# One load of turned keys into another tile, its split at a later slot, and a later place for the memory's PV product

## The chip, the cores and the metric

The kernel runs on one core of a Trainium2 chip. Five engines of that core work side by side, each through its own list of instructions: TensorE (PE in the profile) multiplies matrices into PSUM, VectorE (DVE) and ScalarE (ACT) do the elementwise work, GpSimd (POOL) does small elementwise work and issues some transfers, SyncE (SP) issues the rest. The metric is the time of one execution on the device in microseconds (us), lower is better.

## The reference

Two layers of a decoder trunk on 256 tokens of width 1024, all in float32. Cut to what matters here:

```
for l in range(2):
    h = rms_norm(x, norm_g[l])
    q_a, k_a, v_a, q_h, f_h, i_h, q_m, z = split(h @ w_in[l])       # 1024 x 5120
    o_a = moba_attention(rope(rms_norm(q_a)), rope(rms_norm(k_a)), v_a)   # 8 heads x 64
    o_h = rms_norm(hgrn2_chunkwise(q_h, f_h, i_h, lb[l]))           # 4 heads x 128, gated linear recurrence
    k_m, v_m = split(rms_norm(mem, mem_norm_g[l]) @ w_mem_kv[l])    # 256 memory tokens
    o_m = memory_attention(rms_norm(q_m), rms_norm(k_m), v_m)       # 4 heads x 128
    y = concat([o_a, o_h, o_m]) * silu(z)                           # 256 x 1536
    x = x + y @ w_out[l]
```

With 256 tokens there is a single 256-key block, so MoBA is plain causal attention here.

## The kernel before, in words

Every large product runs in float32r with split operands: a weight tile `wr` (128 x 1024) is loaded by SP, ScalarE rounds it into a high part `wh` (L186, L189), VectorE subtracts that to get the low part `wl` (L198, L201), and TensorE adds three passes, high x high, high x low and low x high. The weights come as 120 such chunks in one fixed order, with 4 buffers for `wr` and 3 each for `wh` and `wl`. Per layer the order is: the memory's keys and values (`group_kv`, 8 chunks), then `FH` and `QH` (forget gate and query of the recurrence, `group_a`), `KA` (MoBA's keys), `IH`, `QA` (MoBA's query), `ZH`, `QM` (the memory's query), `VA`, and the gates `ZA` and `ZM`, 4 chunks each; then 12 chunks of `w_out` (`w_out_phase`), those of the recurrence first, MoBA's next, the memory's last (`KT_ORDER`).

All other work is written as Python generators. `spawn` adds one to a list; each `slot` of the matmul loops calls `step`, which moves every generator on by one; `yield n` waits n slots. So a larger number puts the instructions behind it later in the program. The framework's scheduler then orders the program by its own estimate of times; `keep_in_program_order` (used by `mm_row` too) holds an instruction at its written place. Tiles with the same `tag` share memory, so the next tile of a tag waits until the last reader of the one before is done.

Three of these generators matter here.

- `g_km` (L603) takes the memory's keys from the accumulators into `kn`, normalises them, and turns them: `across` transposes 32 x 32 blocks on VectorE into `blk` (L95), SP writes `blk` to a DRAM buffer `there` (L103) and loads it back in four pieces (L108), so that keys stand along the partitions' other axis. The pieces land in `kn` again. ScalarE then scales them into the high part `kmh` (L632) and VectorE forms the low part `kml` (L633). Their reader is the memory's score product (L1086), after `QM`.
- `g_hgrn` (L758), the recurrence. Its first product chain needs `hQ` (L696) and `hQb` (L799); TensorE's small products with them (L789, recorded at L244) are held at their written place. VectorE carries the pairs on from level to level (L775, L776) between them. Its result goes through the same turning on POOL's queue (`y_turned`), into `zh`, and is split into `yh` and `yl` (L125, L126), the first operand of `w_out`.
- The two PV products of each attention come in units `u` = 0 and 1. MoBA's (L1011) multiplies `va` with the turned probabilities `PT`, which also go through DRAM on POOL's queue. The memory's (L1138) multiplies `vmh` and `vml` with `mP`; its first matmul is held at its written place, which the `yield 4` at L1131 sets. Both write one of four PSUM buffers `sd`; `y_store` (L738) multiplies with the gate and splits the result for `w_out`.

Of the kernel before, what the change touches and what calls it, by code (L numbers as in the profile page):

```python
# [12 lines left out]
F32 = mybir.dt.float32  # L13
F32R = mybir.dt.float32r
# [3 lines left out]
AF = mybir.ActivationFunctionType  # L18
OP = mybir.AluOpType
# [26 lines left out]
def hymba_kernel(ctx: ExitStack, tc: tile.TileContext, x, mem, mem_t, positions, w_in, w_out, w_mem_kv,  # L46
                 gains, moba_g, out):
    nc = tc.nc
    cst = ctx.enter_context(tc.tile_pool(name="cst", bufs=1))
    sb = ctx.enter_context(tc.tile_pool(name="sb", bufs=1))  # L50
# [13 lines left out]
    def room(what, n=1):  # L64
        while held[what] + n > room_of[what]:
            yield
# [9 lines left out]
    def side_tile():  # L76
        held["sd"] += 1
        assert held["sd"] <= 4
        return psum.tile([128, 512], F32, name="sd", tag="sd", bufs=4)

    def rel(what="sd", n=1):
        held[what] -= n

    def small(name, n):
        return sb.tile([128, n], F32, name=name, tag=name, bufs=2)


    def across(dst, src, n, stage=None, free=None, name=None, q=None):
        q = q or nc.sync
        if stage is None:  # L90
            yield from room("blk")
            held["blk"] += 1
        tag = stage or "blk"
        blk = sb.tile([128, 4, n * 32], F32, name="blk", tag=tag, bufs=1)
        nc.vector.transpose(blk.rearrange("p c (n i) -> p c n i", n=n),  # L95
                            src.rearrange("p (n c i) -> p c n i", n=n, c=4))
        if free is not None:
            rel(free)
        if name is not None:
            done.add(name)  # L100
        yield 2
        there = away.tile([4, 32, 4, n * 32], F32, name="there", tag="there", bufs=2)
        q.dma_start(there.rearrange("q j c r -> (q j) c r"), blk)  # L103
        if stage is None:
            rel("blk")
        yield 4
        for c in range(4):
            q.dma_start(dst[c * 32:c * 32 + 32], there[:, :, c].rearrange("q j r -> j q r"))  # L108
            if c == 1:
                yield  # L110

    def turned(a, stage=None, q=None):
        yield from across(a.rearrange("p (q r) -> p q r", q=4), a, 8, stage, q=q)
        yield 5

    def strips(a):
        return a.rearrange("p (q t h i) -> p h t q i", q=4, t=2, h=4)
# [91 lines left out]
    done = set()  # L209
# [29 lines left out]
    def mm(o, a, b, s, e):  # L239
        nc.tensor.matmul(o, lhsT=a, rhs=b, start=s, stop=e)  # L240
# [347 lines left out]
    def heads(t, n):  # L588
        return t.rearrange("p (h d) -> p h d", h=n)

    def sumsq(dst, acc, n):
        sq = sb.tile([128, 512], F32, name="sq", tag="sq", bufs=2)
        nc.scalar.activation(sq, acc, AF.Square)
        nc.vector.tensor_reduce(dst, heads(sq, n), AX.X, OP.add)
# [8 lines left out]
    def g_km(l, acc):  # L603
        ss = small("ssk", 8)
        kn = sb.tile([128, 2, 512], F32, name="kn", tag="qk", bufs=1)
        nc.vector.tensor_copy(kn[:, 0], acc[0])
        nc.scalar.copy(kn[:, 1], acc[1])  # L607
        yield
        for t in range(2):
            sumsq(ss[:, t * 4:t * 4 + 4], kn[:, t], 4)  # L610
        yield
        while "rm" not in done:
            yield
        ms = small("msk", 8)
        for t in range(2):
            nc.vector.tensor_scalar(ms[:, t * 4:t * 4 + 4], ss[:, t * 4:t * 4 + 4], rm2[:, t:t + 1], EPS,
                                    op0=OP.mult, op1=OP.add)
        r = small("rk", 8)
        nc.gpsimd.tensor_tensor(r, ms, pw[:, :8], op=OP.pow)
        for t in range(2):  # L620
            nc.gpsimd.tensor_scalar(r[:, t * 4:t * 4 + 4], r[:, t * 4:t * 4 + 4], rm[:, t:t + 1], None, op0=OP.mult)
        yield 3
        for t in range(2):
            nc.vector.tensor_tensor(heads(kn[:, t], 4), heads(kn[:, t], 4),
                                    r[:, t * 4:t * 4 + 4][:, :, None].to_broadcast([128, 4, 128]), op=OP.mult)
        yield 3
        kmh = sb.tile([128, 1024], F32R, name="kmh", tag="kmh", bufs=1)
        kml = sb.tile([128, 1024], F32R, name="kml", tag="kml", bufs=1)
        g = gkq[:, l:l + 1]
        flat = kn.rearrange("p t s -> p (t s)")  # L630
        yield from turned(flat)
        nc.scalar.activation(kmh, flat, AF.Copy, scale=g)  # L632
        nc.vector.scalar_tensor_tensor(kml, in0=flat, scalar=g, in1=kmh.bitcast(F32), op0=OP.mult, op1=OP.subtract)  # L633
        T["km"] = kmh, kml
        done.add(f"km{l}")

# [437 lines left out]
    def g_mem_unit(l, u, qm, r, nr):  # L1074
        km, vm = T["km"], T["vm"]
        passes = ((0, 1), (1, 0), (0, 0))
        if u == 0:
            yield from room("P")
            held["P"] += 1
        P = sb.tile([128, 2, 2, 256], F32, name="P", tag=("P", "qk")[u], bufs=2 - u)  # L1080
        yield from room("sd", 2)
        ps = [side_tile() for _ in range(2)]
        for t in range(2):
            for i in range(2):
                for a, b in passes:
                    mm(ps[t][:, i * 256:(i + 1) * 256].rearrange("p (t q s) -> p t q s", t=2, q=4),  # L1086
                       qm[a][:, 2 * u + i, t * 128:(t + 1) * 128], strips(km[b])[:, 2 * u + i],
                       (a, b) == passes[0], (a, b) == passes[2])
        done.add(f"scores{u}{l}")
        yield  # L1090
        mx = small("mxm%d" % u, 4)
        nb = small("nbm%d" % u, 4)
        sm = small("smm%d" % u, 4)
        ri = small("rim%d" % u, 4)
        for t in range(2):
            nc.vector.tensor_reduce(mx[:, 2 * t:2 * t + 2], heads(ps[t], 2), AX.X, OP.max)
        nc.vector.tensor_tensor(nb.rearrange("p (t h) -> p t h", t=2), mx.rearrange("p (t h) -> p t h", t=2),
                                nr.rearrange("p (t h) -> p t h", t=2)[:, :, 2 * u:2 * u + 2], op=OP.mult)
        yield
        for t in range(2):  # L1100
            for i in range(2):
                c, cr = 2 * t + i, 4 * t + 2 * u + i
                T["exp"] = nc.scalar.activation(P[:, t, i], ps[t][:, i * 256:(i + 1) * 256], AF.Exp,
                                     bias=nb[:, c:c + 1], scale=r[:, cr:cr + 1], accum_out=sm[:, c:c + 1])
            rel()
            yield
        if u:
            done.add(f"exps{l}")
        yield
        nc.vector.reciprocal(ri, sm)  # L1110
        for t in range(2):
            for i in range(2):
                c = 2 * t + i
                nc.vector.tensor_scalar(P[:, t, i], P[:, t, i], ri[:, c:c + 1], None, op0=OP.mult)
        yield 5
        while f"scores1{l}" not in done:
            yield
        PT = [sb.tile([128, 2, 2, 256], F32R, name="mP", tag=n, bufs=1) for n in (("hF", "kmh"), ("ih", "kml"))[u]]
        for b in range(2):
            yield from room("sd")  # L1120
            pt = side_tile()
            for i in range(2):
                for t in range(2):
                    nc.tensor.transpose(pt[:, i * 256 + t * 128:i * 256 + (t + 1) * 128],
                                        P[:, t, i, b * 128:(b + 1) * 128], ident)
            nc.scalar.copy(PT[0][:, b], heads(pt, 2))
            nc.vector.tensor_tensor(PT[1][:, b], heads(pt, 2), PT[0][:, b].bitcast(F32), op=OP.subtract)
            rel()
        if u == 0:
            rel("P")  # L1130
        yield 4  # L1131
        yield from room("sd")
        po = side_tile()
        for i in range(2):
            hs = slice((2 * u + i) * 128, (2 * u + i + 1) * 128)
            for b in range(2):
                for x, y in passes:
                    (mm if i or b or x != passes[0][0] or y != passes[0][1] else mm_row)(po[:, i * 256:(i + 1) * 256], vm[x][:, b, hs], PT[y][:, b, i],  # L1138
                       b == 0 and (x, y) == passes[0], b == 1 and (x, y) == passes[2])
        yield  # L1140
        while f"z{M_}{l}" not in done:
            yield
        y_store(l, M_, u, po)
# [130 lines left out]
```

## Time and profile before

| | |
|---|---|
| median of 3 runs | 399.3 us (398.44 to 402.74) |
| the profiled execution | 402.14 us, of which the span of its instructions is 400.3 us |
| TensorE busy | 390.2 us (97%) |
| VectorE, ScalarE, GpSimd busy | 314.6, 250.8, 69.7 us |
| mean granted TensorE clock | 0.999 |
| moved by DMA | 80.33 MB, 201 GB/s |

TensorE is busy almost throughout, so a microsecond can only be won where TensorE waits, or at the ends of the span. The profile names each such wait by the instruction that waited and the one that released it.

### The profile page before, as it was taken

To read this page: it belongs to the slowest core of one execution; us is meant where nothing else is said; L and a number is where in the kernel's file an instruction comes from. 1 tells how busy PE (TensorE), PEld (TensorE's weight loads), DVE (VectorE), ACT (ScalarE), POOL (GpSimd) and SP (SyncE) were. 2 spreads that over 40 slices of the span, in tenths; PEclk is the share of its full clock that TensorE was granted. 3 is DMA by queue.
4 is the path that set the end of the run, shared out by engine and by line. 5 is a ranking of instruction groups with operands and counts; after the bars stand their busy time and mean duration, and the time that the engine had idled before them with its cause. 6 is when DMAs were issued, how large, how long until landed. Compare 5 with 4: busy or idle time off the path is not lost.

```text
span 400.3 us, 7603 instructions
## 1 busy us (share of the span) xinstructions
PE 390.2 (97%) x2871; PEld 326.3 (82%) x2871; DVE 314.6 (79%) x606; ACT 250.8 (63%) x422; POOL 69.7 (17%) x109
## 2 busy tenths in 40 slices
PE   8999998999999999899999999999999999989996
PEld 6888887778888888788888888788888889878885
DVE  4789969998559997974576689799866799788543
ACT  5998754646768849644375665455855894875340
POOL 2013400703202514000000040031050061300000
PEclk9999999999999999999999999999999999999999
DMA  7976684368533989726565558554854188981612
GB/s 277 412 281 228 233 213 159 111 210 252 169 106 149 245 288 297 232 86 203 185 196 174 180 189 251 179 176 165 270 187 145 59 265 256 331 245 54 207 56 105
DMA packets 24900, 80.33 MB, mean 201 GB/s; under 512 B 3232, under 2 KB 5664, under 8 KB 24864
## 3 DMA queue, kind: packets, MB, share of 16 engines
q1 hardware_dynamic: 22304, 71.31, 53.5%
q0 software_dynamic: 2272, 8.39, 8.1%
q8 instruction: 22, 0.36, 0.4%
q10 hardware_dynamic: 288, 0.15, 0.1%
q14 instruction: 14, 0.11, 0.1%
HBM read 72.51 MB, written 7.34 MB: 199 GB/s over the span
## 4 chain that ended last, share of the span: by engine, by line
PE 73%; DMA 8%; DVE 8%; issue 4%; POOL 3%; ACT 2%; SPq 1%; ACTq 0%; DVEq 0%; POOLq 0%
PE acc L240 47%; PE acc L1160 16%; PE sd L240 5%; DMA kn<-there 4%; PE sd L244 3%; DMA zh<-there 3%; DVE wl L198 2%; POOL PT L108 1%; POOL rka L900 1%; PE sd L453 1%; DVE blk L95 1%; POOL zh L108 1%; DMA gT<-in_gains_dram 1%; DMA there<-blk 1%; ACT wh L186 1%
## 5 line engine op out<-in xcount | busy, mean ns | idle before, releaser
L198 DVE TENSOR_TENSOR wl<-wr,wh 128x1024 fp32r<-128x1024 f32 x96 | 116.7, 1218 | 42.6 <-ACT wh L186 42.5
L186 ACT CAST wh<-wr 128x1024 fp32r<-128x1024 f32 x96 | 100.5, 1050 | 66.1 <-PE acc L240 35.3
L240 PE MATMUL acc<-wh,hT 128*128 128x512 f32 x384 | 124.8, 396 | 0.0
L240 PEld LDWEIGHTS acc<-wh,hT 128*128 128x128 f32 x384 | 71.8, 188 | 16.1 <-issue 0.7
L240 PE MATMUL acc<-wl,hT 128*128 128x512 f32 x192 | 75.2, 392 | 0.7 <-DVE wl L198 0.7
L240 PE MATMUL acc<-hT,wh 128*128 128x512 f32 x256 | 65.3, 393 | 0.0
L240 PEld LDWEIGHTS acc<-hT,wh 128*128 128x128 f32 x256 | 45.8, 189 | 8.2 <-ACT kn L607 0.4
L240 PEld LDWEIGHTS acc<-wl,hT 128*128 128x128 f32 x192 | 36.1, 188 | 7.9 <-DVE wl L198 1.0
L240 PEld LDWEIGHTS acc<-hT,wl 128*128 128x128 f32 x256 | 35.2, 190 | 2.5
L1160 PE MATMUL acc<-wl,yh 128*128 128x512 f32 (+1 forms) x96 | 37.2, 387 | 0.0
L1160 PE MATMUL acc<-wh,yl 128*128 128x512 f32 (+1 forms) x96 | 36.6, 388 | 0.0
L240 PE MATMUL acc<-hT,wl 128*128 128x256 f32 x256 | 36.6, 283 | 0.0
L201 DVE SCALAR_TENSOR_TENSOR wl<-wr,gT,wh 128x1024 fp32r<-128x1024 f32 (+1 forms) x29 | 31.2, 1097 | 6.7 <-ACT wh L189 6.3
L189 ACT ACTIVATE wh<-wr,gT 128x1024 fp32r<-128x1024 f32 (+1 forms) x29 | 28.6, 1002 | 10.9 <-PE acc L240 4.0
L1160 PE MATMUL acc<-wh,yh 128*128 128x512 f32 (+1 forms) x96 | 30.7, 390 | 2.5 <-ACT yh L125 2.5
L240 PE MATMUL acc<-wh,mTh 128*128 128x512 f32 x64 | 25.4, 401 | 0.2 <-DVE mTh L392 0.2
L240 PE MATMUL acc<-wh,mTl 128*128 128x512 f32 x64 | 25.2, 397 | 0.0
L1160 PEld LDWEIGHTS acc<-wh,yh 128*128 128x128 f32 x96 | 18.0, 188 | 6.6 <-ACT yh L125 3.0
L986 ACT ACTIVATE P<-P,nba,rq 128x128 f32<-128x128 f32 (+1 forms) x32 | 17.1, 536 | 8.3 <-DVE nba L980 8.3
L1160 PEld LDWEIGHTS acc<-wh,yl 128*128 128x128 f32 x96 | 18.0, 188 | 3.8 <-issue 0.2
L1160 PEld LDWEIGHTS acc<-wl,yh 128*128 128x128 f32 x96 | 18.0, 188 | 3.6
L240 PE MATMUL acc<-wl,mTh 128*128 128x512 f32 x64 | 20.2, 392 | 0.0
(222 smaller groups left out, 574.6 us busy)
## 6 DMA issues: line engine op xcount, KB each, us to landing
wr<-in_w_in_dram SPq DMA_DIRECT2D x80, 512.0 KB, 4.2
wr<-in_w_out_dram SPq DMA_DIRECT2D x24, 512.0 KB, 4.6
wr<-in_w_mem_kv_dram SPq DMA_DIRECT2D x15, 512.0 KB, 4.4
there<-blk POOLq DMA_DIRECT2D x4, 768.0 KB, 4.7
PT<-there POOLq DMA_DIRECT2D x16, 192.0 KB, 7.2
there<-blk SPq DMA_DIRECT2D x4, 512.0 KB, 3.1
xs<-in_x_dram SPq DMA_DIRECT2D x2, 512.0 KB, 8.8
memr<-in_mem_dram SPq DMA_DIRECT2D x2, 512.0 KB, 6.7
```

The costliest lines, as they stand in the source:

```text
L95: nc.vector.transpose(blk.rearrange("p c (n i) -> p c n i", n=n), src.rearrange("p (n c i) -> p c n i", n=n, c=4))
L108: q.dma_start(dst[c * 32:c * 32 + 32], there[:, :, c].rearrange("q j r -> j q r"))
L186: nc.scalar.copy(whs[i], raws[i])
L189: nc.scalar.activation(whs[i][:, sl], raws[i][:, sl], AF.Copy, scale=gT[:, g:g + 1])
L198: nc.vector.tensor_tensor(wls[i], raws[i], whs[i].bitcast(F32), op=OP.subtract)
L201: ins = nc.vector.scalar_tensor_tensor(wls[i][:, sl], in0=raws[i][:, sl], scalar=gT[:, g:g + 1], in1=whs[i][:, sl].bitcast(F32), op0=OP.mu ...
L240: nc.tensor.matmul(o, lhsT=a, rhs=b, start=s, stop=e)
L244: tc.keep_in_program_order(nc.tensor.matmul(o, lhsT=a, rhs=b, start=s, stop=e))
L453: ins = nc.tensor.transpose(pt[:, j * 256 + t * 128:j * 256 + (t + 1) * 128], xn[t][:, k * 128:(k + 1) * 128], ident)
L900: nc.gpsimd.tensor_tensor(r[:, t8], ms[:, t8], pw[:, :8], op=OP.pow)
L986: nc.scalar.activation(P[:, i, kc[t]], P[:, i, kc[t]], AF.Exp, bias=nb[:, c:c + 1], scale=rq[:, r:r + 1], accum_out=sm[:, c:c + 1])
L1160: ins = nc.tensor.matmul(a, lhsT=y, rhs=wt[:, cs], start=n == (0 if to is None else nk - 2) and j == 0, stop=n == nk - 1 and j == 2)
```

## The change

In `g_km` the four pieces of the turned keys are loaded into `kt`, a float32 tile in the memory that `kml` has, instead of back into `kn`. ScalarE's scaling and VectorE's subtraction read `kt`; the subtraction writes its result over its own input. Both no longer follow five slots after the load: they wait until `g_ih` has marked the recurrence's input as taken over (`ih{l}`, during `QA`), and five more slots, and are held at that written place. In `g_mem_unit` the memory's PV product stands eight slots after its probabilities instead of four.

```
-        kml = sb.tile([128, 1024], F32R, name="kml", tag="kml", bufs=1)
+        kt = sb.tile([128, 1024], F32, name="kml", tag="kml", bufs=1)
+        kml = kt.bitcast(F32R)
         g = gkq[:, l:l + 1]
-        flat = kn.rearrange("p t s -> p (t s)")
-        yield from turned(flat)
-        nc.scalar.activation(kmh, flat, AF.Copy, scale=g)
-        nc.vector.scalar_tensor_tensor(kml, in0=flat, scalar=g, in1=kmh.bitcast(F32), op0=OP.mult, op1=OP.subtract)
+        yield from across(kt.rearrange("p (q r) -> p q r", q=4), kn.rearrange("p t s -> p (t s)"), 8)
+        while f"ih{l}" not in done:
+            yield
+        yield 5
+        tc.keep_in_program_order(nc.scalar.activation(kmh, kt, AF.Copy, scale=g))
+        tc.keep_in_program_order(nc.vector.scalar_tensor_tensor(kml, in0=kt, scalar=g, in1=kmh.bitcast(F32),
+                                                                op0=OP.mult, op1=OP.subtract))
...
         if u == 0:
             rel("P")
-        yield 4
+        yield 8
         yield from room("sd")
         po = side_tile()
```

The numbers of lines behind L635 grow by four (L799 becomes L803, L1160 becomes L1164). What this does to the order on three engines, layer 0:

On VectorE, near the end of `QH`, the row of `kml` stood ahead of the recurrence's `hQ` and `hQb`. Before:

```order
L324 TENSOR_TENSOR as<-acc,al 128x256
L511 SCALAR_TENSOR_TENSOR rt<-rt 128x16
L633 SCALAR_TENSOR_TENSOR kml<-kn,gkq,kmh 128x1024
L504 TENSOR_SCALAR rt<-rt 128x16
L696 TENSOR_TENSOR hQ<-as,sg 128x512
L505 TENSOR_SCALAR rt<-rt 128x16
L198 TENSOR_TENSOR wl<-wr,wh 128x1024
L799 TENSOR_TENSOR hQb<-hQ,hF 128x1024
```

Now the same stretch, where `rt` are small steps of the rotary angles:

```order
L324 TENSOR_TENSOR as<-acc,al 128x256
L511 SCALAR_TENSOR_TENSOR rt<-rt 128x16
L504 TENSOR_SCALAR rt<-rt 128x16
L505 TENSOR_SCALAR rt<-rt 128x16
L506 TENSOR_SCALAR rt<-rt 128x16
L700 TENSOR_TENSOR hQ<-as,sg 128x512
L511 SCALAR_TENSOR_TENSOR rt<-rt 128x16
L803 TENSOR_TENSOR hQb<-hQ,hF 128x1024
```

The row of `kml` has gone from here, `hQb` stands ahead of the next `wl`, and the small rotary steps have moved forward.

On ScalarE the row of `kmh` now stands during `ZH`, after the two squares of MoBA's query (`sq`) and ahead of `hX`, a copy for the recurrence's output:

```order
L593 ACTIVATE sq<-acc 128x512
L186 CAST wh<-wr 128x1024
L635 ACTIVATE kmh<-kml,gkq 128x1024
L863 COPY hX<-sd 128x512
L186 CAST wh<-wr 128x1024 x2
```

VectorE's row of `kml` follows there too, ahead of a `wl`; both layers have it so.

On TensorE, at the start of `w_out`, unit 0 of the memory's PV (`mP`) came first, then four rows of `w_out` (`yh`), then the memory's unit 1 with MoBA's unit 0 (`PT`) inside it. Before:

```order
L240 MATMUL sd<-mP,vmh 128x256
L1160 MATMUL acc<-wh,yh_1991 128x512
L1160 MATMUL acc<-wl,yh_1991 128x512
L1160 MATMUL acc<-wh,yh_1991 128x512
L1160 MATMUL acc<-wl,yh_1991 128x512
L244 MATMUL sd<-mP,vmh 128x256
L240 MATMUL sd<-mP,vml 128x256
L240 MATMUL sd<-mP,vmh 128x256
L244 MATMUL sd<-PT,va 64x256
L240 MATMUL sd<-PT,va 64x128
```

Now MoBA's unit 0 stands ahead of the memory's unit 0, and both ahead of `w_out`:

```order
L240 MATMUL sd<-PT,va 64x256
L240 MATMUL sd<-PT,va 64x128
L244 MATMUL sd<-mP,vmh 128x256
L240 MATMUL sd<-mP,vml 128x256
L240 MATMUL sd<-mP,vmh 128x256 x2
L240 MATMUL sd<-mP,vml 128x256
L240 MATMUL sd<-mP,vmh 128x256 x2
L240 MATMUL sd<-mP,vml 128x256
L240 MATMUL sd<-mP,vmh 128x256 x2
L240 MATMUL sd<-mP,vml 128x256
L240 MATMUL sd<-mP,vmh 128x256
L1164 MATMUL acc<-wh,yh_1991 128x512
```

Eight matmuls with `PT` have moved ahead of the first row of `w_out`; the memory's unit 1 has moved behind some 30 rows of `w_out`, and MoBA's unit 1 stands alone between rows 8 and 9 of it. Layer 1 has the same shape, with MoBA's unit 1 after row 6.

## The prediction

> **What bounds the kernel now.** The page comes first: which engine is full, and at what clock.
>
> ```profile
> span 400.3 us, 7603 instructions
> PE 390.2 (97%) x2871; PEld 326.3 (82%) x2871; DVE 314.6 (79%) x606; ACT 250.8 (63%) x422; POOL 69.7 (17%) x109
> PEclk9999999999999999999999999999999999999999
> PE 73%; DMA 8%; DVE 8%; issue 4%; POOL 3%; ACT 2%; SPq 1%; ACTq 0%; DVEq 0%; POOLq 0%
> ```
>
> TensorE is busy in 97% of the span at full clock, and the change neither adds nor removes a matmul. So only TensorE's waits can be won: 400.3 - 390.2 = 10.1 us are not busy, start and end included. The last line says that the chain of work that ended last runs over TensorE for 73% only; the rest passes through transfers and VectorE, so some waits are on that chain. The view of waits for TensorE names them (total, times, longest):
>
> ```profile
> PE acc L1160 <- ACT yh L125: 2.5, 2, 1.5
> PE sd L244 <- DVE hQb L799: 1.5, 2, 1.0
> ...
> PE acc L240 <- DVE wl L198: 0.7, 1, 0.7
> PE sd L244 <- DVE hKb L776: 0.5, 1, 0.5
> ```
>
> That is 5.2 us in four kinds, and the timeline of TensorE gives their places (start, duration, and idle time ahead in brackets):
>
> ```profile
> 61.95 0.76 PE L244 MATMUL sd<-hQb,hK 128*32 128x32 f32 x64 [1.01 <-DVE hQb L799]
> ...
> 80.51 0.50 PE L240 MATMUL acc<-wl,hT 128*128 128x512 f32 x1 [0.72 <-DVE wl L198]
> ...
> 88.35 0.65 PE L244 MATMUL sd<-hQ,hKb 128*32 128x64 f32 x32 [0.54 <-DVE hKb L776]
> ...
> 257.72 0.76 PE L244 MATMUL sd<-hQb,hK 128*32 128x32 f32 x64 [0.50 <-DVE hQb L799]
> ...
> 164.38 0.50 PE L1160 MATMUL acc<-wh,yh 128*128 128x512 f32 x1 [1.05 <-ACT yh L125]
> ...
> 358.86 0.50 PE L1160 MATMUL acc<-wh,yh 128*128 128x512 f32 x1 [1.49 <-ACT yh L125]
> ```
>
> Three stand in layer 0 behind the recurrence's first product (1.01 + 0.72 + 0.54 = 2.27), one at the same place in layer 1 (0.50), and one at each start of `w_out` (1.05 + 1.49 = 2.54). Sum 5.31. The first four lead back, on the chain, to the load of the turned keys:
>
> ```profile
> 44.68 2.97 DMA there<-blk
> ...
> 48.99 7.31 DMA kn<-there
> ...
> 244.75 6.86 DMA kn<-there
> ```
>
> and on ScalarE and VectorE, in order of time, to the two instructions that read it:
>
> ```profile
> 56.40 1.15 ACT L632 ACTIVATE kmh<-kn,gkq 128x1024 fp32r<-128x1024 f32 x1 [3.88 <-DMA kn<-there]
> 57.59 1.28 DVE L633 SCALAR_TENSOR_TENSOR kml<-kn,gkq,kmh 128x1024 fp32r<-128x1024 f32 x1 [3.54 <-ACT kmh L632]
> 60.68 1.22 DVE L799 TENSOR_TENSOR hQb<-hQ,hF 128x1024 f32<-128x1024 f32 x1
> ...
> 252.87 1.28 DVE L633 SCALAR_TENSOR_TENSOR kml<-kn,gkq,kmh 128x1024 fp32r<-128x1024 f32 x1 [2.71 <-ACT kmh L632]
> ```
>
> VectorE stood still for 3.54 us with `hQ` and `hQb` queued behind `kml`; TensorE needed `hQb` 1.01 us before it came.
>
> **Part 1, the split moves: four waits go.** In layer 0 the idle 3.54 and the instruction's own 1.28 us leave the stretch, so VectorE can be up to 4.82 us earlier at `hQb`. ScalarE's `sg`, which `hQ` needs, no longer queues behind `kmh` either. TensorE would want VectorE 2.27 us earlier up to 88.35, so 4.82 covers it with 2.5 to spare; beyond that VectorE is held by the `wh` of the chunks, which TensorE paces. VectorE's other work there is the same, only in another order: the rotary steps come early, and POOL makes the rotary table before its two slow powers. In layer 1 it is 2.71 + 1.28 = 3.99 against 0.50. I take both as won whole: **2.77 us**; the ends are 0 (POOL's powers hold VectorE instead) and 2.77.
>
> **Where the two instructions go.** They now stand in `ZH`, ahead of the rows below. The load has landed some 40 us earlier by then, so they wait for nothing; behind them on ScalarE stand `hX` and the next `wh`, behind them on VectorE the next `wl`.
>
> ```profile
> 97.02 0.58 ACT L859 COPY hX<-sd 128x512 f32<-128x512 f32 x1
> 99.69 1.05 ACT L186 CAST wh<-wr 128x1024 fp32r<-128x1024 f32 x1 [2.09 <-PE acc L240]
> ...
> 103.50 1.22 DVE L198 TENSOR_TENSOR wl<-wr,wh 128x1024 fp32r<-128x1024 f32 x1 [1.50 <-ACT wh L186]
> ...
> 115.04 2.68 PE sd L240 x24
> ...
> 171.12 31.07 PE acc L1160 x136
> ```
>
> ScalarE has 2.09 us of idle time behind `hX` for its 1.15; VectorE gives 1.28 out of 1.50. `hX`, which TensorE reads in the stretch from 115.04 on, was ready at 97.6, so 1.15 later is free. Cost **0**; without that cover it is at most 1.28 per layer, which is the upper end. The four loads themselves keep their place on SP's queue; they only write another tile, whose last reader in layer 0 is nothing and in layer 1 the memory's unit 1 of layer 0: at 31.07 / 136 = 0.23 us a row it ends some 30 rows and three PV products behind 164.4, near 175, against a load near 240. Cost 0, both ends.
>
> **Part 2, MoBA's unit 0 moves into the wait.** The start of `w_out` is set by `zh`:
>
> ```profile
> 132.44 2.24 POOL L108 DMA_DIRECT2D PT<-there  x4 [1.54 <-PE acc L240]
> ...
> 157.02 0.56 POOL L108 DMA_DIRECT2D zh<-there  x1 [2.52 <-issue]
> ...
> 157.02 6.60 DMA zh<-there
> 163.71 0.63 ACT yh L125
> ...
> 351.98 6.11 DMA zh<-there
> DMA to landing us min/median/max: 5.6/7.2/9.2
> ```
>
> The last row is that of `PT`: issued until 134.7 and landing at most 9.2 us later, unit 0's probabilities are there by 143.9, long before TensorE is done with `ZM` and takes up the memory's unit 0, at 161.73 in the next rows. So the moved matmuls wait for nothing. Their length:
>
> ```profile
> 161.73 0.28 PE L244 MATMUL sd<-mP,vmh 128*128 128x256 f32 x1
> ...
> 163.05 0.28 PE L240 MATMUL sd<-mP,vmh 128*128 128x256 f32 x1
> ...
> 165.86 0.43 PE L244 MATMUL sd<-PT,va 128*64 128x256 f32 x1
> ...
> 167.36 0.39 PE L240 MATMUL sd<-mP,vmh 128*128 128x256 f32 x1
> ```
>
> 167.36 - 165.86 = 1.50 us. Layer 0's wait of 1.05 is filled whole (TensorE then comes 0.45 after `yh`, less the 0.17 of a matmul's ordinary spacing); layer 1's 1.49 is filled to within nothing. I take 1.05 + 1.49 = **2.54 us**, provided `zh` comes earlier by as much as TensorE does. For that, one row of busy times (TensorE, weight loads, VectorE, ScalarE, POOL) and two of the timeline: from 120 to 142 VectorE is full on the way to `zh` and `PT`, but the work that leads into this stretch waits for TensorE:
>
> ```profile
> 120.00:142.00 22.00, 22.00 (x117) 18.82 (x116) 21.96 (x60) 16.31 (x35) 7.75 (x8) 1.00 0.72 202
> ...
> 104.69 0.59 ACT L936 COPY qT<-sd 128x512 f32<-128x512 f32 x1 [0.73 <-PE sd L935]
> 107.22 0.69 DVE L719 TENSOR_TENSOR zh<-acc,sg 128x512 f32<-128x512 f32 x1 [2.49 <-ACT sg L717]
> ```
>
> So the stretch begins earlier by what TensorE has won, and `zh` follows. The memory's unit 1 comes some 7 us later; its result is wanted by the last third of `w_out`, some 66 rows of 0.23 us behind. Cost 0; the upper end is in the third rival.
>
> **The sum.** 2.77 + 2.54 = 5.31. I keep 0.7 of it back for waits this small that shift rather than go: the new order leaves the low part `yl` a few tenths only before its first reader, at both starts of `w_out`. Gain **4.6 us**. The profiled execution took 402.14 (span 400.3 and 1.84 around it), so 397.5 on its own footing. It stands 2.84 above the median of 399.3. If a profiled run carries that always, the median becomes 394.7. For this speaks that the waits recur alike in both layers, so they are not one run's accident.
>
> A rule of the Trainium skill speaks against part 2. "DMA: Bandwidth & Descriptors", in "Anatomy of one DMA", fits POOL-issued transfers as 2.0 us and bytes at 436 GB/s; by it the last piece of `zh` (128 KB) would land about 2.3 us after its issue, an estimate, ahead of TensorE, part 2 would win nothing, and the sum would be 2.77 alone, 396.5. The trace disagrees: 6.60 and 6.11 us.
>
> **The rivals.**
> 1. *The waits were larger in the profiled execution than in the median one.* Landing times of `kn` (7.31, 6.86) and `zh` set them, and transfers vary: the three runs spread over 4.3 us while TensorE's work is fixed. Then the change reaches a floor that the median had half reached: 402.14 - 5.31 = 396.8. Against it: the like waits in both layers. 0.24. The rule of the skill's page would be the extreme of this case, with its 396.5.
> 2. *`zh` does not follow TensorE.* VectorE is full from 120 to 142; if its own work and not its start sets the end, `w_out` starts when it does now, and what is won ahead of it is given back as a longer wait. Each layer then wins only the 1.50 of unit 0, which no longer stands behind: 3.0, hence 396.3. A new hold in layer 0 (VectorE waiting for POOL's powers at `kr`) gives about the same, 5.31 - 2.27 = 3.0. 0.18.
> 3. *Slower: `zh` comes later.* TensorE runs ahead, and the loads of weights crowd the same 16 DMA engines as `PT` and `zh`. The fourth piece of `zh` is issued when the first piece of unit 1's `PT` has landed (the 2.52 us marked issue), so both latencies count. At the 9.2 of the view instead of 6.60 and 6.11 the last piece costs 2.6 and 3.1 us, and the `PT` piece ahead of it up to 3.0 and 2.2 more: 10.9 in all, less 5.3, so 399.3 + 5.6 = 404.9. It decides from 5.3 us over both layers on. Against it: the rows are from the same crowded stretches. 0.08.
> 4. *It does not do what it says*, and the scheduler's new order trades one wait for another: within 1 us of 399.3. 0.06.
>
> **How the numbers follow.** The forecast holds 0.44, with 394.7; its own range is 393.4 (all 5.31 and another 0.1 us of slower restart behind each of six waits) to 396.8. The range over the cases is 393.4 to 399.0: it leaves out the third rival and part of the fourth. About 1% (4.0 us) can be told from no change in this kernel: faster than 395.3 is most of the forecast and a little of the first two rivals, 0.44; slower than 403.3 is the third rival, 0.07; the rest, 0.49.
>
> **What would show it.** In the changed profile TensorE's waits on `hQb`, `hKb` and `wl` should be gone in both layers; `kmh` should have no wait on a transfer and stand near 97 and 289; TensorE should pass from `ZM` through `PT` and `mP` into `yh` with under 0.3 us idle. It is wrong if the wait on `yh` stays over 1 us (rival 2 or 3), if VectorE waits for POOL at `kr` near 68, or if TensorE waits for the fourth chunk's `wh` or `wl` in `w_out`, whose buffers come free only with chunk 0's last row, now about a dozen rows later.

## The result, and the profile after

| | before | after |
|---|---|---|
| median | 402.3 us (20 runs, 398.44 to 407.19) | 396.43 us (20 runs, 395.34 to 399.69) |
| ratio | | 0.9877, 95% interval 0.9852 to 0.9902 |
| the profiled execution | 402.14 us | 399.69 us, the longest of its 20; a second one 398.48 us |

The change wins 1.2%, some 5 us by the ratio and 5.9 by the medians. (A ratio, here and below, is over the fast executions alone, those within 1.5% of the kernel's lowest time; a median is over all of them.) The forecast was 394.7 us; the range held the time. The 399.3 us of the three runs shown before lay 3 us under what the same kernel does over many runs (402.3 here; 402.11, 402.28 and 402.33 beside the experiments).

The page of the profile after, in the places that answer to those of before:

```profile
span 397.9 us, 7596 instructions
PE 390.5 (98%) x2871; PEld 326.1 (82%) x2871; DVE 314.6 (79%) x606; ACT 251.1 (63%) x422; POOL 70.3 (18%) x109
PE 86%; DMA 4%; DVE 4%; POOL 2%; issue 2%; ACT 1%; SPq 0%; ACTq 0%; DVEq 0%; POOLq 0%
```

TensorE's share of the chain that ended last has gone from 73 to 86%; DMA and VectorE have 4% each instead of 8%. The view of waits for TensorE:

```profile
PE acc L1164 <- ACT yh L125: 2.0, 1, 2.0
PE sd L240 <- DVE dm L368: 1.0, 1, 1.0
PE acc L240 <- DVE mTh L392: 0.3, 1, 0.3
PE acc L240 <- ACT wh L189: 0.2, 1, 0.2
PE sd L244 <- ACT wh L186: 0.2, 1, 0.2
```

The lines on `hQb`, `hKb` and `wl` are gone; `dm`, `mTh` and `wh` belong to the first 9 us of the program, and the last line is all that is left in the recurrence. TensorE's timeline has the three places of layer 0 where it waited before, then the way from `ZM` to the start of `w_out`, then the start of `w_out` in layer 1:

```profile
60.73 0.71 PE L244 MATMUL sd<-hQb,hK 128*32 128x32 f32 x62
...
78.38 0.49 PE L240 MATMUL acc<-wl,hT 128*128 128x512 f32 x1
...
85.82 0.65 PE L244 MATMUL sd<-hQ,hKb 128*32 128x64 f32 x32 [0.17 <-ACT wh L186]
...
159.28 0.43 PE L244 MATMUL sd<-PT,va 128*64 128x256 f32 x1
...
160.78 0.39 PE L244 MATMUL sd<-mP,vmh 128*128 128x256 f32 x1
...
162.31 0.40 PE L1164 MATMUL acc<-wh,yh 128*128 128x512 f32 x1
...
356.51 0.79 PE L1164 MATMUL acc<-wh,yh 128*128 128x512 f32 x1 [2.01 <-ACT yh L125]
```

Rows without a bracket waited for nothing. In layer 0 TensorE goes from `ZM` through `PT` and `mP` into `yh` without a pause, 2.45 us earlier than before at the first row behind `ZM` (161.73 there). In layer 1 of this execution it waits longer than before, 2.01 instead of 1.49. A second profile of the same kernel has it the other way round, a wait in layer 0 and none in layer 1:

```profile
164.74 0.50 PE L1164 MATMUL acc<-wh,yh 128*128 128x512 f32 x1 [1.84 <-ACT yh L125]
...
353.83 0.43 PE L244 MATMUL sd<-PT,va 128*64 128x256 f32 x1
...
356.87 0.40 PE L1164 MATMUL acc<-wh,yh 128*128 128x512 f32 x1
```

The chains of the two executions name the reason, the last piece of `zh` (start, duration to landing). The first execution, layer 1, then the second, layer 0:

```profile
345.52 10.21 DMA zh<-there
```

```profile
156.38 7.59 DMA zh<-there
```

Before it took 6.60 and 6.11. In the first execution the piece itself took long, and so did its three neighbours (13.0 to 13.3 us); in the second it was also issued late, 5.4 us behind the first piece of `zh` (150.98) where it was 4.2 before, since it is the eighth transfer of GpSimd's queue and came only when the first piece of `PT` had landed. So the cover of part 2 is enough where `zh` lands as before, and some executions have a landing that goes beyond it. Both profiled executions have the longest time of their group, while 16 of the 20 runs lie between 395.3 and 397.0. The same is true of all three runs below that have both parts in another form: whether the profiled execution is longer because it is profiled, or by its place in the run, is not known.

A sum without these two waits: in the chains, layer 0 can be followed from a row near 24 us, behind the program's start, and layer 1 begins with the second row shown. Before,

```profile
24.25 19.25 PE acc L240 x103
...
202.19 10.66 PE acc L240 x47
```

and now:

```profile
24.21 36.03 PE acc L240 x188
...
198.36 10.66 PE acc L240 x47
```

From equal starts (24.25 and 24.21) that is 3.8 us for layer 0, where 2.27 + 1.05 = 3.32 were predicted. For layer 1 the second execution, which did not wait there, has 191.8 us from its chain's same row to TensorE's last one, the profile before 194.2: 2.4 us, where 0.50 + 1.49 = 1.99 were predicted. Together 6.2, and 402.14 - 6.2 = 395.9, where most runs are.

```profile
200.89 10.66 PE acc L240 x47
...
392.70 0.28 PE L1164 MATMUL sd<-wh,yl 128*128 128x256 f32 x1
```

(Before, the second of these rows starts at 396.39.) That is 0.9 us more than the six idle times, and the timelines place it. Up to the first row behind `ZM` the layers have become 2.41 and 0.64 us shorter (137.48 to 135.07, 153.58 to 152.94) where 2.27 and 0.50 were idle: 0.28 more. From there to the layer's end, with the waits taken off, 39.41 has become 39.08 and 39.13 has become 38.87: another 0.59 for the same matmuls in another order.

### The profile page after: what moved, and what is told of

Its sections match the earlier page's. It is cut to its first block, busy times and chain, and to the rows that moved or that the text cites. A ratio compares the mean times of both kernels' runs of the same rounds, so it can differ in the third digit from the quotient of the medians.

```text
span 397.9 us, 7596 instructions
## 1 busy us (share of the span) xinstructions
PE 390.5 (98%) x2871; PEld 326.1 (82%) x2871; DVE 314.6 (79%) x606; ACT 251.1 (63%) x422; POOL 70.3 (18%) x109
## 4 chain that ended last, share of the span: by engine, by line
PE 86%; DMA 4%; DVE 4%; POOL 2%; issue 2%; ACT 1%; SPq 0%; ACTq 0%; DVEq 0%; POOLq 0%
PE acc L240 58%; PE acc L1164 17%; PE sd L240 5%; PE sd L244 3%; DMA zh<-there 3%; DMA wr<-in_w_mem_kv_dram 1%; DVE wl L198 1%; PE sd L453 1%; ACT wh L186 1%; POOL rka L904 1%; POOL PT L108 0%; PE sd L1068 0%; PE sd L939 0%; PE sd L1128 0%; POOL rtB L548 0%
## 5 line engine op out<-in xcount | busy, mean ns | idle before, releaser
L1164 PE MATMUL acc<-wl,yh 128*128 128x512 f32 (+1 forms) x96 | 37.7, 392 | 0.0
L1164 PE MATMUL acc<-wh,yl 128*128 128x512 f32 (+1 forms) x96 | 37.1, 392 | 0.0
L1164 PE MATMUL acc<-wh,yh 128*128 128x512 f32 (+1 forms) x96 | 30.4, 396 | 2.0 <-ACT yh L125 2.0
L1164 PEld LDWEIGHTS acc<-wh,yh 128*128 128x128 f32 x96 | 18.3, 190 | 6.1 <-ACT yh L125 2.2
L1164 PEld LDWEIGHTS acc<-wh,yl 128*128 128x128 f32 x96 | 18.3, 191 | 3.8
L1164 PEld LDWEIGHTS acc<-wl,yh 128*128 128x128 f32 x96 | 18.3, 191 | 3.6
```

The lines of the kernel that those rows point to most:

```text
L1164: ins = nc.tensor.matmul(a, lhsT=y, rhs=wt[:, cs], start=n == (0 if to is None else nk - 2) and j == 0, stop=n == nk - 1 and j == 2)
```

## The experiments

Each part was run by itself, against the prices of 2.77 us for the split and 2.54 us for the cover, and against the rival that `zh` does not follow.

### The split alone (two runs)

The change, with the memory's PV in `g_mem_unit` at its old place:

```
-        yield 8
+        yield 4
```

> The split of kn alone: new tile and late place as in the change, but the memory's PV four slots behind its probabilities as before, so that the start of w_out has its old order on TensorE. My theory (the four waits behind the load go whole, and zh follows TensorE): the waits on hQb, hKb and wl are gone, the wait for yh stays at 1.0 to 1.3 us in layer 0 and near 1.5 in layer 1, and the time falls by 2.8 us, ratio 0.993. Rival 2 (zh does not follow): the same waits go, but the wait for yh grows to about 3.3 us in layer 0 and 2.0 in layer 1, ratio 1.000. If the median execution has smaller waits than the profiled one: 0.995 to 0.998.

Measured: 401.47 us at the median (398.0 to 406.3 without the profiled execution), ratio 0.9971, 0.9936 to 1.0006. The profiled execution of this run was out of order as a whole (1366.95 us), so the kernel was run again for its profile.

> The split of kn alone once more, now to see its profile: its runs fell into a group near 398.4 and one near 401.8 us. Theory A (the gate): TensorE waits for yh at the start of w_out some 1.5 to 2.5 us in one layer or both, and where the wait fills more than half of one window of 3.41 us the clock is 0.50 in the window behind it, which costs 1.7 us more each time; ratio again 0.996 to 0.998. Theory B (zh does not follow, no gate): the wait grows to 3.3 and 2.0 us and the clock stays at 1.00.

Measured: 401.0 us, ratio 0.9954, 0.9916 to 0.9993; the profiled execution took 399.09. Its waits, without those of the first 9 us and 0.17 us on a `wh`:

```profile
PE acc L1164 <- ACT yh L125: 2.1, 2, 1.6
```

The waits behind the load are gone, and in this execution (1.64 and 0.42 us at `yh`) `zh` has followed; the clock stayed at 1.00. So neither A nor B is what the profile shows. Yet of the 2.77 us the median gained only 0.6 in the first run and 1.3 in the second (1.2 and 1.9 by the ratios), and it lies 2 us above the execution that was profiled. What the other executions lose had to be found by taking suspects away.

### The place of the memory's PV alone

The kernel before, with this one line of the change:

```
-        yield 4
+        yield 8
```

> The PV's place alone: split of kn as before, the memory's PV eight slots behind its probabilities, so that MoBA's unit 0 stands ahead of w_out. My theory (MoBA's unit 0 fills the wait for zh, 1.05 and 1.49 us): the wait for yh goes in both layers, the waits on hQb, hKb and wl stay as they were, the time falls by 2.5 us, ratio 0.994. If the two parts only pay together (the cover needs part 1): 1.000. If nearly all of the whole gain comes from here, since a late zh also costs clock: 0.989 to 0.991.

Measured: 399.42 us, ratio 0.9959, 0.9921 to 0.9998; 2.7 us at the median and 1.6 by the ratio, beside the 2.54 of the sum. TensorE's waits behind the first 9 us:

```profile
PE acc L1160 <- ACT yh L125: 2.0, 1, 2.0
PE sd L244 <- DVE hQb L799: 0.6, 1, 0.6
PE sd L244 <- DVE hKb L776: 0.6, 1, 0.6
PE acc L240 <- DVE wl L198: 0.5, 1, 0.5
```

Behind `kml` three of the four waits are there (layer 0's on `hQb` is missing in this execution), and the wait for `yh` has left layer 0. In layer 1 this execution, too, met a late `zh`.

By the ratios the split alone gives 1.2 to 1.9 us, the PV's place 1.6, both together 4.9. That they pay more together than apart is suggested by this and not shown: each ratio has an interval of some 1.5 us either way.

### Only the tile

The kernel before, with `kt` as in the change and the two instructions at their old place:

```
-        yield from turned(flat)
-        nc.scalar.activation(kmh, flat, AF.Copy, scale=g)
-        nc.vector.scalar_tensor_tensor(kml, in0=flat, scalar=g, in1=kmh.bitcast(F32), op0=OP.mult, op1=OP.subtract)
+        yield from across(kt.rearrange("p (q r) -> p q r", q=4), kn.rearrange("p t s -> p (t s)"), 8)
+        yield 5
+        nc.scalar.activation(kmh, kt, AF.Copy, scale=g)
+        nc.vector.scalar_tensor_tensor(kml, in0=kt, scalar=g, in1=kmh.bitcast(F32), op0=OP.mult, op1=OP.subtract)
```

> Only the tile: the turned keys land in kml's tile and the two instructions read it, at the old place in the program (five slots behind the load, not held), all else as before. My theory (only the place counts, the tile is a means): VectorE still stands 3 us or more in front of kml with hQb behind it, ratio 1.000 within 0.002. Rival (the target of the load matters, because loading into kn waits for its last reader): the load of the pieces starts earlier or lands sooner, and a part of the 2.8 us goes, ratio 0.995 or less.

Measured: 402.79 us, ratio 1.003, 0.9998 to 1.0063. ScalarE and VectorE still stand in front of the landing, with the queue behind them:

```profile
55.62 1.15 ACT L633 ACTIVATE kmh<-kml,gkq 128x1024 fp32r<-128x1024 f32 x1 [2.58 <-DMA kml<-there]
56.81 1.29 DVE L634 SCALAR_TENSOR_TENSOR kml<-kml,gkq,kmh 128x1024 fp32r<-128x1024 f32 x1 [2.25 <-ACT kmh L633]
```

The rival falls: the tile by itself brings nothing. Keeping `kn` as the load's target with a late split was not tried, because MoBA's keys take over `kn`'s memory in between.

### The split soon behind the load, alone and with part 2

The split alone, with another place for it:

```
-        while f"ih{l}" not in done:
-            yield
-        yield 5
+        yield 9
```

> The tile, with the split held nine slots behind the load and no waiting for the recurrence's input: kml stands on VectorE behind the first hQb (two levels further on) in KA, some 40 us earlier than in the change; the memory's PV as before. My theory (what counts is that hQ and hQb no longer stand behind the load; how far the split moves is indifferent): like the split alone, ratio 0.993. Rival (the late place counts, because VectorE has no room for 1.28 us in the recurrence's levels): TensorE waits on hQb or hKb of a later level by up to 1.3 us in each layer, ratio 0.996 to 1.000.

Measured: 398.93 us, ratio 0.9914, 0.9875 to 0.9954, with

```profile
PE acc L1162 <- ACT yh L125: 2.1, 2, 1.5
```

as the only wait of TensorE behind the start. The interval overlaps those of the late split (0.9971, 0.9954), so a difference is not shown. With the PV's new place besides:

> The split nine slots behind the load, held (as in the run of that name, 0.991 alone), with the memory's PV eight slots behind its probabilities as in the change. If the place of the split does not matter as long as it is behind hQb: the same as the change, ratio to before 0.986 to 0.989. If the late place in ZH costs something on the way to zh (the split alone gave 0.997 there, against 0.991 here): 1 to 2 us below the change, ratio 0.982 to 0.985.

Measured: 396.19 us, ratio 0.9857, 0.9811 to 0.9903, the change's own time. As far as these runs can tell, how late the split stands does not matter; that it stands behind `hQb` does. (The profiled execution, 398.18 us, waited 1.49 us for `yh` in layer 1.)

### The new place's cover

The change, with two more instructions between its own two:

```
+        tc.keep_in_program_order(nc.scalar.activation(kmh, kt, AF.Copy, scale=g))
+        ex = sb.tile([128, 1024], F32R, name="ex", tag="ex", bufs=1)
+        tc.keep_in_program_order(nc.vector.scalar_tensor_tensor(ex, in0=kt, scalar=g, in1=kmh.bitcast(F32),
+                                                                op0=OP.mult, op1=OP.subtract))
```

> The change, with both instructions of the split issued twice at their new place: a second kmh (the same values) and a second low part into a tile of its own, so 1.15 us more on ScalarE and 1.28 more on VectorE in each layer. The prediction put the cost of the new place at 0, because ScalarE is idle for 2.09 us behind hX and VectorE for 1.50 ahead of wl there. If the cover holds with room: the same as the change within 0.5 us, ratio 0.985 to 0.989. If the cover is already used up: up to 1.28 us a layer on TensorE's path, 398 to 399, ratio 0.990 to 0.993, and the profile shows TensorE waiting for wh, wl or hX between 95 and 120 us.

Measured: 396.39 us, ratio 0.9859, 0.9824 to 0.9894. VectorE and ScalarE did the work twice,

```profile
94.49 1.15 ACT L635 ACTIVATE kmh<-kml,gkq 128x1024 fp32r<-128x1024 f32 x1
...
96.01 1.15 ACT L636 ACTIVATE kmh<-kml,gkq 128x1024 fp32r<-128x1024 f32 x1
```

```profile
98.38 1.28 DVE L638 SCALAR_TENSOR_TENSOR ex<-kml,gkq,kmh 128x1024 fp32r<-128x1024 f32 x1
...
100.71 1.28 DVE L640 SCALAR_TENSOR_TENSOR kml<-kml,gkq,kmh 128x1024 fp32r<-128x1024 f32 x1
```

and TensorE waited for nothing between 95 and 120 us. The cover holds with room for as much again. (At `yh` in layer 1 this execution, 397.41 us, waited 1.25.)

### Is it the clock? Matmuls of zeros in the wait

Two profiles (below, on the hardware) show a stretch of half clock behind a wait for `yh` of 2.0 us. If such stretches make up what the split alone loses (theory A), keeping TensorE busy in the wait must win it back. The split alone, and in `w_out_phase`, ahead of the first rows:

```
+            if n == 0:
+                for _ in range(10):
+                    mm_row(acc[0][0][:, :256], zb[:, :128], zb)
```

> The split of kn alone, and ten matmuls of zeros (128x256, about 0.11 us each, 1.1 in all) into an accumulator just ahead of the memory's unit 0 at each start of w_out; they change no result, for the first row of w_out starts that accumulator anew. They do nothing for the time at which yh is there. Theory A (a part of the price of the late zh is the clock that falls after it): TensorE is idle 1.1 us less, the clock does not fall any more, and the time is 1.5 to 2.5 us below that of the split alone, ratio to before 0.991 to 0.993, with a narrower spread. Theory B (only the wait counts): the same as the split alone where the wait is over 1.1 us, and up to 1.1 us per layer more where it is shorter: 0 to 1.5 us above the split alone.

Measured: 400.88 us (399.57 to 404.25), ratio 0.9988, 0.9955 to 1.002, beside 401.0 (from 397.74) and 0.9954 for the split alone in the same session. The lowest time rose by 1.8 us, nearly the ten matmuls' length over two layers (1.03 us a layer in the profile), and the median did not move. So the gain of 1.5 to 2.5 us that theory A asked for did not come, and theory B's numbers fit.

The clock is not cleared by this, for the record has the mean granted clock of every execution. Of 23 executions of the split alone, 13 have a clock of 0.996 or less; none has 0.997. The medians of these 13 are 402.0 and 401.7 us in the two runs, those of the others 398.6 and 399.1. One window at half clock, 1.7 us in 400, is 0.4%. With the ten matmuls only 2 of 12 are so low. The falls went, as theory A has it, but the ten matmuls cost an execution without a fall 1.6 to 2.1 us (the median of such executions is now 400.7), and the median of all stays. So the median execution of the split alone loses a wait and a window of half clock behind it, and this experiment does not part the two.

### zh ahead of PT on GpSimd's queue

The direct test of a late `zh` is to make it early. In `across` the four loads of unit 1's `PT` come three slots later (`lag` is 7 for it and 4 for all others) and are held there; the product with `PT` keeps its slot, since its own `yield 13` becomes 10:

```
-        yield 4
+        yield lag
...
-            q.dma_start(dst[c * 32:c * 32 + 32], there[:, :, c].rearrange("q j r -> j q r"))
+            ins = q.dma_start(dst[c * 32:c * 32 + 32], there[:, :, c].rearrange("q j r -> j q r"))
+            if pin:
+                tc.keep_in_program_order(ins)
```

First with the whole change, then with the split alone, then with the kernel before.

> The change, and the four loads of unit 1's PT are issued three slots later and held there, so that the four loads of zh stand ahead of them on GpSimd's queue. The scheduler then takes four rows of w_out ahead of MoBA's unit 0. If the late fourth piece of zh, which waits for the first piece of PT to land, is what is left at the start of w_out: zh lands 3 to 4 us earlier, no wait on yh is left, MoBA's unit 1 gets its PT in time, and the time is 0 to 1 us below that of the change (ratio to before 0.984 to 0.987), with no run near 399. Rival: the bytes on the DMA engines set the landing, not the order of issue: zh lands hardly earlier, the four rows that now come first wait, and TensorE then waits for PT as well, 0.5 to 3 us above the change.

Measured: 395.98 us (395.74 to 396.71), ratio 0.9839, 0.9793 to 0.9886. GpSimd's timeline and TensorE's first row of `w_out` in layer 1:

```profile
150.32 2.24 POOL L108 DMA_DIRECT2D zh<-there  x4 [6.45 <-DMA there<-blk]
152.72 1.67 POOL L108 DMA_DIRECT2D PT<-there  x3 [0.17 <-issue]
155.48 0.56 POOL L108 DMA_DIRECT2D PT<-there  x1 [1.09 <-issue]
```

```profile
351.98 0.40 PE L1166 MATMUL acc<-wh,yh 128*128 128x512 f32 x1
```

Now the eighth transfer, the one held back, is a piece of `PT`; `zh` has landed 2.7 to 2.9 us before TensorE takes up `yh`, and the row waits for nothing, in either layer. No run is over 396.71. This is the lowest median of all; 0.4 to 0.6 us below the change's medians is less than these runs can tell.

> The split of kn alone (the memory's PV four slots behind its probabilities), and the four loads of zh ahead of those of unit 1's PT on GpSimd's queue. The split alone gave 401.2 at the median, though its profile (399.09) shows 2.06 us of waiting for yh and a floor of 397.0. Theory C (in the median execution the rest up to 401 is waiting for a late zh): with zh early it goes without part 2 of the change, 396 to 397, ratio 0.984 to 0.987, narrow. Theory D (the rest is somewhere else): only the 2.06 go, 399 to 399.5, ratio 0.991 to 0.993.

Measured: 397.25 us (396.9 to 397.66), ratio 0.9881, 0.985 to 0.9912. Theory C has the cause right and the number a little low: without part 2, 3.8 of the split's 401.0 us go (2.9 by the ratios), though its profile showed only 2.06 us of waiting. No execution has a clock of 0.996 or less any more, so what goes is the wait and the half clock behind it. TensorE's waits behind the first 9 us are down to one line:

```profile
PE sd L246 <- ACT wh L188: 0.2, 1, 0.2
```

It still lies 1.3 us over the same with part 2, where neither waits for `yh`. Most of this is the order of the rows in `w_out`: from its first row to the row with which layer 1 begins, the chain's second one below, the split with `zh` first takes 39.66 us,

```profile
159.73 0.40 PE L1166 MATMUL acc<-wh,yh 128*128 128x512 f32 x1
...
199.39 10.66 PE acc L242 x47
```

and the change with `zh` first 39.19:

```profile
159.99 0.40 PE L1166 MATMUL acc<-wh,yh 128*128 128x512 f32 x1
...
199.18 10.66 PE acc L242 x47
```

The same matmuls take 0.47 us less in this layer and 0.46 in the other (39.44 against 38.98 to the last row), together 0.9 of the 1.3. That it is because the memory's unit 1 isn't broken off for `PT` is a guess.

> The kernel before (split at its old place, the memory's PV four slots behind its probabilities), with the four loads of zh ahead of those of unit 1's PT on GpSimd's queue. This takes the waits at w_out away and leaves those behind kml. Step 1 of the prediction says that these cost 2.77 us over both layers, against the run of the split with zh first: 399.2 to 399.6, ratio 0.993. If the waits behind kml are given back later whenever they go (rival 2 in another form): the same as with the split, 396 to 397.

Measured: 399.45 us (397.02 to 401.3), ratio 0.9933, 0.9902 to 0.9965. This is the expected number. The waits for `yh` are gone, those behind `kml` are whole, 3.10 us in this execution:

```profile
PE sd L246 <- DVE hQb L801: 1.3, 2, 0.8
...
PE acc L242 <- DVE wl L200: 0.7, 1, 0.7
PE sd L246 <- DVE hKb L778: 0.6, 1, 0.6
PE sd L246 <- DVE hQ L698: 0.5, 1, 0.5
```

### The change once more

> The change as it is, for a second profile. The first one was the slowest of its 20 executions (399.69): a wait of 2.01 us at the second start of w_out and a window of half clock behind it. If that was an accident of one execution: no wait over 1 us in either layer, span near 394.5, median 396.4, ratio 0.985 to 0.989.

Measured: 396.62 us (396.06 to 398.48), ratio 0.9873, 0.9838 to 0.9907. The profile is the second execution shown above. Half of the expectation fails: a wait at one start of `w_out` is no accident of one execution, but comes again, now in one layer, now in the other.

### All medians in one table

| us, and ratio to before | split at its old place | split moved |
|---|---|---|
| PV after 4 slots | 402.3 (before) | 401.47 (0.9971), 401.0 (0.9954); soon behind the load 398.93 (0.9914) |
| PV after 8 slots | 399.42 (0.9959) | 396.43 (0.9877), 396.62 (0.9873) (the change); soon behind the load 396.19 (0.9857) |
| PV after 4, `zh` first | 399.45 (0.9933) | 397.25 (0.9881) |
| PV after 8, `zh` first | not run | 395.98 (0.9839) |

Read by the ratios, the split is worth 1.2 to 1.9 us where a late `zh` meets TensorE at `w_out` (3.5 in the run with the split soon behind the load), 2.1 where `zh` is early, 3.3 to 3.5 where MoBA's unit 0 stands in the wait. Each of these has some 2 us of interval either way, so their order is not shown. The granted clocks speak more plainly: 0.996 or less in 41 of 76 executions of the kernel before, 13 of 23 of the split alone, 3 of 12 of the PV's place alone, 1 of 26 of the change, and none of the 24 with `zh` first.

## Why the prediction was right, and where it was not

**Part 1, the split moves: right.** None of the four waits is there in any profile with the split moved. The profiles without it show 2.77 us (before), 1.73, 2.00 and 3.10, so the size differs from one execution to the next. By itself the split measures 1.2 to 1.9 us (3.5 in the run with the split soon behind the load). That the second rival holds there in part, TensorE coming earlier and the `zh` of the median execution not, fits the falls of the clock but not the profile, where `zh` had followed; it is not shown. The prediction gave that rival 0.18 as a case of the whole change; the whole change has the cover against it.

**The new place costs nothing: right.** `kmh` waits for no transfer, and the same work twice is free too. The instructions stand at 94.5 and 286.5, a few us earlier than forecast (97, 289), as the whole layer does.

**A new hold of VectorE did come,** of the sort that was named as a sign of error:

```profile
73.70 0.23 DVE L909 TENSOR_TENSOR tm<-acc,rtB 128x64 f32<-128x64 f32 x1 [1.75 <-POOL rtB L547]
```

VectorE waits 1.75 us for GpSimd's rotary table, 6 us later than guessed. TensorE does not lose by it (its one pause there, 0.17 us at 85.82, is put down to ScalarE's `wh`): 1.75 lay inside the slack of 2.5 that the step had named.

**Part 2, MoBA's unit 0 in the wait: right in kind, mis-sized.** Priced at 2.54, it measures 1.6 us alone by the ratio (2.7 by the median) and 3.1 to 3.8 (4.6 to 4.8) on top of the split. The sum did not have two terms of it: the order of rows, some 0.3 us a layer, and the clock, which fell in 41 of 76 executions before and in 1 of 26 after, at up to 1.7 us a fall. "Filled to within nothing" is wrong as a statement on every execution: in the two profiles of the change, the sign "under 0.3 us idle" is there at two of the four starts profiled, and the other two waited 2.01 and 1.84 us, over the 1 us that was named as proof of rival 2 or 3. It was neither: both come from a landing beyond the cover, and other executions have none. TensorE waited nowhere for the fourth chunk's `wh` or `wl`.

**The 0.7 us kept back: wrong in sign.** No such waits came back, and 0.9 us more went than the idle times, two thirds of it by the order of rows; the prediction's lower end had allowed 0.1 a wait. On the profiled execution's footing 397.5 was forecast and 395.9 is what the undisturbed stretches add up to, 1.6 lower.

**The footing: the step that failed.** The profiled execution was taken to stand 2.84 us above the median, "always". Over 20 runs the median of before is 402.3, and 402.14 stood on it. This error of 3.0 us downward and the one of 1.3 to 1.6 upward made 394.7 out of a true 396.4. The first rival names 396.8, close by, for a reason that stays open: the profiled execution had the median's time, but no fall of the clock (0.999), while half of the others had one; among those without, whose medians are 400.4 to 401.3 in the three sessions, it is a long one. The small draw was low: two of its three runs are among the four lowest of the 20. That 394.7 came within 2 us is partly luck, since the two errors have opposite signs.

**Slower (third rival), and no effect (fourth):** excluded by the interval. The landing that the third one feared does occur, in the profiles in one layer at a time, and it does not eat the gain.

By the Trainium skill's "DMA: Bandwidth & Descriptors", "Anatomy of one DMA", `zh` would land 2.3 us behind its issue (an estimate), and moving it ahead or covering it would win nothing. The runs disagree: by the ratios either one, where the other is absent, wins 1.6 to 3.8 us, and the last piece of `zh` landed 6.1 to 10.2 us behind its issue.

**What stays open:** why `zh` comes later in many executions of the split alone than in the one that was profiled (3.8 us of the median vanish with `zh` first, 2.06 were seen). That the loss hangs on `zh` is shown by taking it away, and the clocks say that a window of half clock is part of it; how much is wait and how much is clock, and which transfers delay `zh` there, was not seen.

## What to carry to other kernels

Time won ahead of a meeting with a transfer can be lost there again, in a wait and in the clock that falls behind it: price the parts of such a change together, test them as a table of two by two, and read the granted clock of every execution beside its time. Work that needs nothing belongs ahead of the row that waits for a landing, and the transfer that is wanted first belongs first on its queue; either made up for most of the other here. Where waits hang on landings, three runs can miss the median by 3 us of 400, as much as the change itself is worth.

## What the runs showed of the hardware that was not expected

**A wait of 2 us can halve the clock of the 3.41 us behind it.** Below are windows of 3.41 us in the profile after, the first ending where the clock falls (window, its length, TensorE's busy time, weight loads, VectorE, ScalarE, GpSimd, the granted clock, DMA):

```profile
352.99:356.41 3.42, 1.51 (x12) 1.31 (x12) 0.44 (x1) 0.57 (x2) 0.00 (x0) 1.00 0.89 320
356.42:359.82 3.40, 3.31 (x8) 2.12 (x10) 3.33 (x6) 3.12 (x7) 0.00 (x0) 0.50 0.06 23
359.83:363.24 3.41, 3.41 (x25) 2.75 (x22) 3.41 (x7) 1.93 (x4) 0.00 (x0) 1.00 0.45 153
```

The same in the PV's place alone, where the wait ended 1.4 us before the clock fell:

```profile
356.77:360.18 3.41, 1.42 (x7) 1.05 (x6) 1.38 (x3) 2.03 (x5) 0.00 (x0) 1.00 0.21 79
360.19:363.60 3.41, 3.41 (x19) 2.10 (x18) 3.41 (x6) 2.23 (x4) 0.00 (x0) 0.50 0.00 0
```

And in the second execution of the change, with 1.84 us of waiting of which 1.6 fell into one window, and no fall:

```profile
161.08:164.49 3.41, 1.82 (x16) 1.49 (x12) 1.68 (x4) 0.42 (x1) 0.00 (x0) 1.00 0.99 290
164.50:167.91 3.41, 3.17 (x20) 2.38 (x22) 3.19 (x5) 2.63 (x5) 0.00 (x0) 1.00 0.09 35
```

Busy for 1.42 and 1.51 of 3.41 us, the next window ran at 0.50; busy for 1.82, it did not. The split alone had a window with 1.80 and no fall either. The windows keep a grid: the trace of the change has its clock rise at 4.84 us and fall at 356.41, 103 times 3.413 us later, that of the PV's place alone at 5.20 and 360.19, 104 times; in the second execution of the change, with the rise at 4.07, a window begins 46 windows later, at 161.08. So the limit lies between 1.51 and 1.80 us, and half a window would fit. A wait of 2.0 us can cost up to 1.7 more, by where it falls in a window: from the first row with `PT` to the last row of `w_out`, layer 1 took 42.62 us with 2.01 of waiting and the half clock, and 38.87 with neither. The Trainium skill's "TensorE: Matmul & The Clock Gate" has the free-running window of about 3.4 us ("Part 1: The HAM clock gate") and warns of idle gaps over about 3.4 us ("HAM oscillation — how this bites in real kernels"). These two gaps were shorter.

**Eight transfers on GpSimd's queue.** Whatever stood eighth, counted from the four pieces of unit 1's `PT` or of `zh`, was issued 0.3 us behind the landing of the first of them: the fourth piece of `zh` at 153.77 behind 153.46 in the profile after, the fourth of `PT` at 155.48 behind 155.18 with `zh` first. It is 0.30 to 0.31 us in both layers of all 13 profiles that are in order. The order of issue thus decides which transfer has two latencies to bear. With `zh` first its pieces also land sooner behind their own issue: 4.3 to 6.2 us, against 5.8 to 13.3 in the other profiles.
